# A prompt delta rule's triangular inverse: 32-blocks joined by 32x32 products in two column groups, and the last join sent to both column halves

## The chip, the cores and the metric

The kernel runs on one core of a Trainium2 chip. A core has TensorE (matrix products, results into PSUM), VectorE, ScalarE, GpSimd, and SyncE, which mostly issues DMAs. The metric is the time of one execution on the device in microseconds; the number compared is the median over runs. A profiled execution is one more run, recorded by the hardware profiler, and its own time differs a little from that of the timed runs.

## The reference

One decoder layer for a prompt of 1024 tokens and for 8 samples of 4 tokens: a combined projection, a stick-breaking attention (8 heads of 64) beside a gated delta rule (4 heads of 128), a merge, and a channel mixer. What matters here is the delta rule of the prompt. The reference works it out in chunks:

```python
def step(s, inp):
    qc, kc, vc, gc, bc = inp
    cg = jnp.cumsum(gc, axis=-1)
    decay = jnp.exp(jnp.where(incl, cg[..., :, None] - cg[..., None, :], -jnp.inf))
    m = jnp.where(strict, bc[..., :, None] * jnp.einsum('bhik,bhjk->bhij', kc, kc) * decay, 0.0)
    rhs = jnp.concatenate([vc * bc[..., None], kc * (bc * jnp.exp(cg))[..., None]], axis=-1)
    sol = lax.linalg.triangular_solve(eye + m, rhs, left_side=True, lower=True, unit_diagonal=True)
    u, w = sol[..., :d_v], sol[..., d_v:]
    v_new = u - jnp.einsum('bhck,bhkv->bhcv', w, s)
    ...
```

The solve with I + m, m strictly lower triangular, is the part that the change touches. All inputs and outputs are float32.

## The kernel before, in words

The prompt's 1024 tokens are 8 chunks of 128, and the kernel inverts I + M for a whole chunk of 128 at once, so that the solve becomes products. For each of the four heads (gdn_head, h from 0 to 3):

- Projections (proj, with its helper dense at lines 137 to 139) make k, q, v and the gate z of the head. Their matmuls are named pd_uk, pd_uq, pd_uv, pd_z.
- M for the 8 chunks stands in one tile (E1 in the code, E in the profile), 128 partitions by 8 x 128.
- The four diagonal 32x32 blocks of every chunk are inverted on VectorE by substitution (lines 471 and 473), in a layout that takes two trips through DRAM (tiles ms and tv). The result, block diagonal, comes back in t32 (t in the profile), and U is its transpose by blocks (line 491).
- The join from 32 to 64 is two steps. Step one (line 500) multiplies U's odd blocks by M under a mask (ml, line 495), full 128x128 products with 64 columns streamed, one per chunk; ScalarE copies the result out (xf, line 501). Step two (line 504) multiplies by t32 in the same form; VectorE subtracts the result from U (line 505), and a transpose and a copy (lines 507 and 508) bring the new block into t32.
- The join from 64 to 128 is steps three and four (lines 511 and 517): products of 64x64, all written to PSUM partitions 0 to 63, with ScalarE's copy x2 between (line 514) and VectorE's copy into U after (line 519).
- With U done, the chain over the 8 chunks follows (lines 526 to 555), the norm, the transposes t_o, the gating zl, and a store.

In the profile the four steps' PSUM tiles are all called l, and a float32 product appears as two MATMUL records.

The order of the instructions is not the order of the code. A planner at build time simulates the program with its own costs and fixes each engine's order; each engine then runs its queue in that order and waits by semaphores. So the matmuls of the next head's projections, and of the attention's (pd_aq, pd_ak, pd_av with their transposes t_nk, t_nv), stand between the steps of the joins on TensorE. PSUM is eight banks, two per pool: the joins take theirs from the pool psg, the projections from psd and psf. On VectorE, ql is the difference that empties a bank of the query projection; qe (cgb in the profile, line 488) is q times an exponential, whose tile is loaded by DMA after the tile's earlier contents, zl of the head before, were stored.

Of the kernel before, what the change touches and what calls it, by code (L numbers as in the profile page):

```python
# [8 lines left out]
F32 = mybir.dt.float32  # L9
# [4 lines left out]
ALU = mybir.AluOpType  # L14
# [4 lines left out]
P = 128  # L19
# [19 lines left out]
def hybrid_step(ctx, tc, x_prompt, x_sample, cache_k, cache_v, page_table, state_conv, state_ssm,  # L39
# [211 lines left out]
    lmask = gk.tile([P, P], F32, name="lmask")  # L251
    V.memset(lmask, 0.0)
    V.memset(lmask[32:64, 0:32], 1.0)
    V.memset(lmask[96:128, 64:96], 1.0)
# [125 lines left out]
    def c8(ap):  # L380
        return ap.rearrange("p (c f) -> p c f", f=P)

    def odd(ap):
        return ap.rearrange("p (a b f) -> p a b f", b=2, f=32)[:, :, 1, :]

    def gdn_head(h):
# [107 lines left out]
        ml = gk.tile([P, NC, P], F32, tag="ms", name=f"ml{h}")  # L494
        V.tensor_tensor(ml, c8(M), lmask.unsqueeze(1).to_broadcast([P, NC, P]), op=ALU.mult)
        xf = gk.tile([P, NP], F32, tag="tv", name=f"xf{h}")
        G.memset(xf, 0.0)
        p1 = gtile(f"l1{h}")
        for c, sl in enumerate(cs_):
            PE.matmul(p1[:, 64 * c:64 * c + 64], lhsT=ml[:, c, :], rhs=odd(U[:, sl]), start=True, stop=True)  # L500
        S_.activation(odd(xf), p1.rearrange("p (a f) -> p a f", f=32), AF.Copy)
        p2 = gtile(f"l2{h}")
        for c, sl in enumerate(cs_):
            PE.matmul(p2[:, 64 * c:64 * c + 64], lhsT=t32[:, sl], rhs=odd(xf[:, sl]), start=True, stop=True)
        V.tensor_tensor(odd(U), odd(U), p2.rearrange("p (a f) -> p a f", f=32), op=ALU.subtract)
# [3 lines left out]
        p3 = gtile(f"l3{h}")  # L509
        for c in range(NC):  # L510
            PE.matmul(p3[0:64, 64 * c:64 * c + 64], lhsT=M[64:128, c * P:c * P + 64], rhs=c8(U)[64:128, c, 64:128],
                      start=True, stop=True)
        x2 = gk.tile([64, 512], F32, tag="x2", name=f"x2{h}")
        S_.activation(x2, p3[0:64, :], AF.Copy)
        p4 = gtile(f"l4{h}")
        for c in range(NC):
            PE.matmul(p4[0:64, 64 * c:64 * c + 64], lhsT=c8(t32)[0:64, c, 0:64], rhs=x2[:, 64 * c:64 * c + 64],
                      start=True, stop=True)
        V.tensor_scalar(c8(U)[0:64, :, 64:128], p4[0:64, :].rearrange("p (a f) -> p a f", f=64), -1.0, None, op0=ALU.mult)
# [1143 lines left out]
```

## Time and profile before

| | |
|---|---|
| median of 3 runs | 1745.63 us (1745.23 to 1746.56) |
| profiled execution | 1754.63 us, span of its instructions 1752.9 us |
| TensorE busy | 1704.8 us, 97% of the span, 13902 records |
| VectorE, ScalarE, GpSimd busy | 1148.9, 783.2, 206.6 us |
| mean granted TensorE clock | 0.992 |

A busy TensorE in this table is a sum over records whose spans overlap, so it tells that the engine had work, not how fast it worked. PE is TensorE's matmul row, PEld its weight loads, DVE is VectorE, ACT ScalarE, POOL GpSimd. The names behind an instruction are its output and inputs; 64*64 is rows by columns of the weights.

### The profile page before, as it was taken

How to read it: one execution, taken by the hardware profiler on the slowest of the kernel's cores; microseconds unless marked ns; L12 is line 12 of the kernel's file. 1: busy time of each engine (PE TensorE's matmuls, PEld its weight loads, DVE VectorE, ACT ScalarE, POOL GpSimd, SP SyncE). 2: the span in 40 equal slices, each digit the busy share in tenths (PEclk: the TensorE clock that was granted, in tenths of full speed). 3: DMA queues.
4: the chain of work that ended last, by engine and by line, in shares of the span. 5: the costliest groups of instructions: out<-in, count | busy, mean ns of one | idle time of the engine just before them, and what ended most of it. 6: DMA issues, size and time to landing. Idle time of an engine off the chain costs nothing.

```text
span 1752.9 us, 34523 instructions
## 1 busy us (share of the span) xinstructions
PE 1704.8 (97%) x13902; PEld 1645.2 (94%) x13902; DVE 1148.9 (66%) x2299; ACT 783.2 (45%) x1554; POOL 206.6 (12%) x247
## 2 busy tenths in 40 slices
PE   7999999999998999999999999999999999999998
PEld 6999999999998787887989999999999999999998
DVE  6665677868224416658857487887777678788843
ACT  5553435343323225555433355554544564444353
POOL 1110111110004125335310000000000000000000
PEclk9999999999998999999999999999999999999999
DMA  5142232234337457758223644554443666532321
GB/s 177 37 127 67 67 117 79 81 96 144 118 97 230 138 161 210 188 145 248 67 86 117 194 126 146 164 150 148 146 150 133 212 215 220 170 123 90 128 83 66
DMA packets 234219, 239.22 MB, mean 136 GB/s; under 512 B 22882, under 2 KB 192195, under 8 KB 234060
## 3 DMA queue, kind: packets, MB, share of 16 engines
q1 hardware_dynamic: 229110, 226.27, 42.4%
q0 software_dynamic: 3200, 10.52, 1.9%
q8 instruction: 109, 1.79, 0.4%
q10 hardware_dynamic: 1750, 0.23, 0.1%
q14 instruction: 50, 0.41, 0.1%
HBM read 163.21 MB, written 73.77 MB: 135 GB/s over the span
## 4 chain that ended last, share of the span: by engine, by line
PE 74%; issue 8%; DMA 6%; DVE 6%; POOL 3%; ACT 1%; SPq 1%; POOLq 0%; DVEq 0%; ACTq 0%
PE pu L139 6%; PE pu L137 6%; PE pu L138 6%; PE pw L139 4%; PE pw L138 4%; PE pw L137 4%; PE pd_g L137 2%; POOL am L938 2%; PE pd_g L139 2%; PE pd_g L138 2%; POOL s L935 1%; PE px L138 1%; PE px L137 1%; PE px L139 1%; PE pv L137 1%
## 5 line engine op out<-in xcount | busy, mean ns | idle before, releaser
L139 PE MATMUL pu<-Xh,ul 128*128 128x264 f32 x812 | 230.1, 284 | 0.0
L137 PE MATMUL pu<-Xh,uh 128*128 128x264 f32 x812 | 229.8, 283 | 0.1
L138 PE MATMUL pu<-Xl,uh 128*128 128x264 f32 x812 | 229.7, 283 | 0.0
L137 PE MATMUL pw<-hc,w 128*128 128x264 f32 x728 | 205.4, 285 | 2.4 <-ACT w L1475 2.4
L138 PE MATMUL pw<-hc,w 128*128 128x264 f32 x728 | 205.7, 286 | 0.0
L139 PE MATMUL pw<-hc,w 128*128 128x264 f32 x728 | 200.9, 285 | 1.0 <-DVE w L1476 1.0
L137 PEld LDWEIGHTS pu<-Xh,uh 128*128 128x128 f32 x812 | 153.1, 189 | 0.3 <-ACT uh L1226 0.3
L137 PE MATMUL pd_g<-xh,wh_g 128*128 128x256 f32 (+1 forms) x512 | 150.9, 295 | 1.8 <-ACT gt L1037 1.6
L138 PEld LDWEIGHTS pu<-Xl,uh 128*128 128x128 f32 x812 | 152.7, 188 | 0.0
L139 PEld LDWEIGHTS pu<-Xh,ul 128*128 128x128 f32 x812 | 152.0, 188 | 0.0
L139 PE MATMUL pd_g<-xh,wl_g 128*128 128x256 f32 (+1 forms) x512 | 149.2, 291 | 0.1
L138 PE MATMUL pd_g<-xl,wh_g 128*128 128x256 f32 (+1 forms) x512 | 148.6, 290 | 0.0
L137 PEld LDWEIGHTS pw<-hc,w 128*128 128x128 f32 x728 | 137.9, 190 | 2.6 <-ACT w L1475 2.6
L138 PEld LDWEIGHTS pw<-hc,w 128*128 128x128 f32 x728 | 137.2, 189 | 0.0
L139 PEld LDWEIGHTS pw<-hc,w 128*128 128x128 f32 x728 | 134.4, 188 | 1.4 <-DVE w L1476 1.4
L942 DVE TENSOR_TENSOR_SCAN pr<-am 128x127 f32<-128x127 f32 (+7 forms) x64 | 88.1, 1378 | 54.8 <-POOL am L938 54.8
L137 PEld LDWEIGHTS pd_g<-xh,wh_g 128*128 128x128 f32 x512 | 97.8, 191 | 7.0 <-ACT gt L1037 3.0
L139 PEld LDWEIGHTS pd_g<-xh,wl_g 128*128 128x128 f32 x512 | 97.6, 191 | 2.0 <-issue 1.9
L138 PEld LDWEIGHTS pd_g<-xl,wh_g 128*128 128x128 f32 x512 | 97.6, 191 | 0.6 <-issue 0.4
L1475 ACT ACTIVATE w<-a 128x512 fp32r<-128x512 f32 x78 | 43.5, 620 | 84.5 <-PE pw L139 74.4
L139 PE MATMUL px<-mh,wl_wo 128*128 128x264 f32 x256 | 72.2, 285 | 0.9 <-DVE wl_wo L1227 0.8
L138 PE MATMUL px<-ml,wh_wo 128*128 128x264 f32 x256 | 72.6, 285 | 0.0
(584 smaller groups left out, 5126.2 us busy)
## 6 DMA issues: line engine op xcount, KB each, us to landing
hc_d<-t SPq DMA_DIRECT2D x26, 924.0 KB
hc<-hc_d SPq DMA_DIRECT2D x87, 264.0 KB
a<-in_w_down_dram SPq DMA_DIRECT2D x48, 256.0 KB
ws_g<-in_w_in_dram SPq DMA_DIRECT2D x16, 512.0 KB
ws_wo<-in_w_o_dram SPq DMA_DIRECT2D x32, 256.0 KB
ua<-in_w_up_dram SPq DMA_DIRECT2D x16, 512.0 KB
ub<-in_w_up_dram SPq DMA_DIRECT2D x16, 512.0 KB
gA_d<-gt SPq DMA_DIRECT2D x8, 528.0 KB
```

The source lines that it names most:

```text
L137: PE.matmul(pt[:, :n], lhsT=wh[k], rhs=xh[k], start=(k == 0), stop=False)
L138: PE.matmul(pt[:, :n], lhsT=wh[k], rhs=xl[k], start=False, stop=False)
L139: PE.matmul(pt[:, :n], lhsT=wl[k], rhs=xh[k], start=False, stop=(k == nk - 1))
L935: G.affine_select(s[:, qsl], s[:, qsl], pattern=[[-1, P]], compare_op=ALU.is_gt, fill=0.0, base=0, channel_multiplier=1)
L938: G.tensor_scalar(am[:, :n], s[:, :n], -1.0, 1.0, op0=ALU.mult, op1=ALU.add)
L942: V.tensor_tensor_scan(pr[:, n - 1:0:-1], am_r, am_r, 1.0, op0=ALU.mult, op1=ALU.bypass)
L1475: S_.activation(tl[:, 0], src, AF.Copy)
```

## The change

Steps one and two become products of 32x32: per chunk two of them, one for each half of 64, with weights in row groups 1 and 3 (step one) or 0 and 2 (step two), written to PSUM partitions 0 to 31 and 64 to 95, which are column groups 0 and 2. The mask and the masked copy of M go, and so does the memset of xf. The copies between the steps become two of 32 partitions each. Steps three and four keep their 64x64 products but write even chunks to PSUM partitions 0 to 63 and odd chunks to 64 to 127; their copies become two as well.

```diff
-        ml = gk.tile([P, NC, P], F32, tag="ms", name=f"ml{h}")
-        V.tensor_tensor(ml, c8(M), lmask.unsqueeze(1).to_broadcast([P, NC, P]), op=ALU.mult)
-        xf = gk.tile([P, NP], F32, tag="tv", name=f"xf{h}")
-        G.memset(xf, 0.0)
-        p1 = gtile(f"l1{h}")
-        for c, sl in enumerate(cs_):
-            PE.matmul(p1[:, 64 * c:64 * c + 64], lhsT=ml[:, c, :], rhs=odd(U[:, sl]), start=True, stop=True)
-        S_.activation(odd(xf), p1.rearrange("p (a f) -> p a f", f=32), AF.Copy)
-        p2 = gtile(f"l2{h}")
-        for c, sl in enumerate(cs_):
-            PE.matmul(p2[:, 64 * c:64 * c + 64], lhsT=t32[:, sl], rhs=odd(xf[:, sl]), start=True, stop=True)
-        V.tensor_tensor(odd(U), odd(U), p2.rearrange("p (a f) -> p a f", f=32), op=ALU.subtract)
+        xf = gk.tile([P, NC, 32], F32, tag="tv", name=f"xf{h}")
+        p1, p2 = gtile(f"l1{h}").rearrange("p (c f) -> p c f", f=64), gtile(f"l2{h}").rearrange("p (c f) -> p c f", f=64)
+        halves = [(slice(64 * a, 64 * a + 32), slice(64 * a + 32, 64 * a + 64)) for a in range(2)]
+        for c in range(NC):
+            for ra, rb in halves:
+                PE.matmul(p1[ra, c, 0:32], lhsT=c8(M)[rb, c, ra], rhs=c8(U)[rb, c, rb], start=True, stop=True)
+        for ra, rb in halves:
+            S_.activation(xf[ra], p1[ra, :, 0:32], AF.Copy)
+        for c in range(NC):
+            for ra, rb in halves:
+                PE.matmul(p2[ra, c, 0:32], lhsT=c8(t32)[ra, c, ra], rhs=xf[ra, c, :], start=True, stop=True)
+        for ra, rb in halves:
+            V.tensor_scalar(c8(U)[ra, :, rb], p2[ra, :, 0:32], -1.0, None, op0=ALU.mult)
...
+        def at(pt, c):
+            return pt[64 * (c % 2):64 * (c % 2) + 64, 64 * (c // 2):64 * (c // 2) + 64]
+
+        def both(pt, r):
+            return pt[64 * r:64 * r + 64, 0:256].rearrange("p (c f) -> p c f", f=64)
+
+        def every(ap, r):
+            return ap.rearrange("p (c r) f -> p r c f", r=2)[:, r]
...
-            PE.matmul(p3[0:64, 64 * c:64 * c + 64], lhsT=M[64:128, c * P:c * P + 64], rhs=c8(U)[64:128, c, 64:128],
-                      start=True, stop=True)
-        x2 = gk.tile([64, 512], F32, tag="x2", name=f"x2{h}")
-        S_.activation(x2, p3[0:64, :], AF.Copy)
...
+            PE.matmul(at(p3, c), lhsT=M[64:128, c * P:c * P + 64], rhs=c8(U)[64:128, c, 64:128], start=True, stop=True)
+        for r in range(2):
+            S_.activation(every(x2, r), both(p3, r), AF.Copy)
         for c in range(NC):
-            PE.matmul(p4[0:64, 64 * c:64 * c + 64], lhsT=c8(t32)[0:64, c, 0:64], rhs=x2[:, 64 * c:64 * c + 64],
-                      start=True, stop=True)
-        V.tensor_scalar(c8(U)[0:64, :, 64:128], p4[0:64, :].rearrange("p (a f) -> p a f", f=64), -1.0, None, op0=ALU.mult)
+            PE.matmul(at(p4, c), lhsT=c8(t32)[0:64, c, 0:64], rhs=x2[:, c, :], start=True, stop=True)
+        for r in range(2):
+            V.tensor_scalar(every(c8(U)[0:64, :, 64:128], r), both(p4, r), -1.0, None, op0=ALU.mult)
```

Since the planner orders the engines, the change also moves work that it doesn't name. On TensorE, in the projection of the next head's k, step two of head 0 stood like this before (l is its PSUM tile, xf and t its inputs):

```order
L138 MATMUL pd_uk_2_2465<-xl_170,wh_uk_2409 128x256
L139 MATMUL pd_uk_2_2465<-xh_169,wl_uk_2410 128x256
L504 MATMUL l_1242<-xf_1230,t_1202 128x64 x8
L137 MATMUL pd_uk_2_2465<-xh_169,wh_uk_2409 128x256
L138 MATMUL pd_uk_2_2465<-xl_170,wh_uk_2409 128x256
```

and stands like this now, where line 498 is step two:

```order
L139 MATMUL pd_uk_2_2495<-xh_169,wl_uk_2440 128x256
L137 MATMUL pd_uk_2_2495<-xh_169,wh_uk_2439 128x256
L498 MATMUL l_1226<-xf_1224,t_1198 32x32
L138 MATMUL pd_uk_2_2495<-xl_170,wh_uk_2439 128x256
L498 MATMUL l_1226<-xf_1224,t_1198 32x32 x15
L139 MATMUL pd_uk_2_2495<-xh_169,wl_uk_2440 128x256
```

The block of 8 has become one product, a dense matmul, and 15 products. Step two of head 3 and step four of heads 1, 2 and 3 (line 522) are parted in the same way, with 1 to 18 dense matmuls between the first product and the others.

On TensorE around step one of head 2, before (t_o are the transposes of the head before, t_nv those of the attention's v, pd_aq the attention's query projection):

```order
L111 MATMUL t_o_1_2389<-ident,nw_2164 128x128 x2
L111 MATMUL t_nv_0_5381<-ident,vf_5268 128x128 x4
L500 MATMUL l_3106<-U_3099,ml_3102 128x64 x8
L111 MATMUL t_nv_1_5386<-ident,vf_5268 128x128 x4
L137 MATMUL pd_aq_0_5403<-xh_173,wh_aq_5399 128x256
```

and now, with step one at line 493:

```order
L139 MATMUL pd_av_3_5417<-xh_167,wl_av_5336 128x288
L111 MATMUL t_nv_0_5445<-ident,vf_5332 128x128 x4
L493 MATMUL l_3133<-U_3129,E_2943 32x32 x16
L111 MATMUL t_nv_1_5450<-ident,vf_5332 128x128 x4
L498 MATMUL l_3134<-xf_3132,t_3106 32x32 x16
L137 MATMUL pd_aq_0_5467<-xh_173,wh_aq_5463 128x256
```

Step two, which stood 22 dense matmuls behind those transposes, now follows them at once, and 19 dense matmuls of the projection pd_av have come between the transposes t_o and step one. From there to the first matmul of pd_aq's third chunk there were 48 dense matmuls before and are 67 now, and the first product of step four stands among them.

## Rows read from the trace of the kernel before

**Rows 1.** The table of busy times by stretch, for 40 to 530 us; the columns are the stretch, its length, busy us and count of PE, PEld, DVE, ACT and POOL, the granted TensorE clock as a share, the DMA share and GB/s.

```profile
40.00:530.00 490.00, 482.34 (x4021) 476.93 (x4020) 301.65 (x736) 193.53 (x435) 55.28 (x52) 1.00 0.31 93
```

**Rows 2.** What TensorE waited for from 60 to 530 us: us in total, times, longest.

```profile
PE pd_aq L137 <- DVE ql L794: 2.4, 1, 2.4
PE pd_uv L137 <- ACT upv L346: 1.1, 1, 1.1
PE t_nk L111 <- ACT ntk L804: 1.1, 2, 0.9
PE s L544 <- DVE y L540: 1.1, 1, 1.1
PE l L500 <- DVE U L491: 0.9, 1, 0.9
PE pd_av L137 <- DVE ksT L798: 0.6, 1, 0.6
PE wt L527 <- DVE kb L526: 0.2, 1, 0.2
```

**Rows 3.** The instructions that write or read U: steps one and three, with duration in ns (least, median, most), first and last start, and form.

```profile
L500 PE MATMUL l<-U,ml x64: 220/275/294, 163.8 to 445.3; 128*128 128x64 f32 x64
...
L511 PE MATMUL l<-U,E x64: 218/218/267, 173.7 to 454.6; 64*64 64x64 f32 x64
```

**Rows 4.** TensorE in order of time around step one of head 0: start, us to the end of the last, instruction, count.

```profile
163.72 0.28 PE L138 MATMUL pd_uk<-xl,wh_uk 128*128 128x256 f32 x1
163.84 1.90 PE L500 MATMUL l<-U,ml 128*128 128x64 f32 x16
...
165.75 0.28 PE L137 MATMUL pd_uk<-xh,wh_uk 128*128 128x256 f32 x1
165.86 0.28 PE L138 MATMUL pd_uk<-xl,wh_uk 128*128 128x256 f32 x1
```

**Rows 5.** The same around step three of head 0.

```profile
173.34 0.30 PE L137 MATMUL pd_uk<-xh,wh_uk 128*128 128x288 f32 x1
173.48 0.29 PE L138 MATMUL pd_uk<-xl,wh_uk 128*128 128x288 f32 x1
173.71 1.14 PE L511 MATMUL l<-U,E 64*64 64x64 f32 x16
...
175.01 0.30 PE L137 MATMUL pd_uk<-xh,wh_uk 128*128 128x288 f32 x1
```

**Rows 6.** The same view, cut to stretches inside steps one and three of head 0, so that only whole records at the running pace are in a row.

```profile
163.90 1.61 PE L500 MATMUL l<-U,ml 128*128 128x64 f32 x13
...
173.87 0.86 PE L511 MATMUL l<-U,E 64*64 64x64 f32 x12
```

**Rows 7.** Products on parts of the array elsewhere in the kernel. First the views by tile, with durations in ns (least, median, most): the decode's dks on four column groups, dav with 32x32 weights on four, dst with 32 rows on four row groups. Then rows in order of time, cut to the first few records of a block: dks, its weight loads, dav, dst, and the attention's po, which alternates between two column halves.

```profile
L723 PEld LDWEIGHTS dks<-sst,kz x128: 106/110/155, 555.4 to 575.5; 128*32 128x32 f32 x128
L723 PE MATMUL dks<-sst,kz x128: 269/273/421, 555.4 to 575.6; 128*32 128x128 f32 x128
...
L893 PE MATMUL dav<-vs_nat,dwn x16: 587/600/612, 620.4 to 639.2; 32*32 32x512 f32 x16
...
L766 PE MATMUL dst<-vexp,dkp x16: 587/640/692, 591.6 to 607.1; 32*128 32x512 f32 x16
...
572.13 0.32 PE L723 MATMUL dks<-sst,kz 128*32 128x128 f32 x4
...
572.13 0.13 PEld L723 LDWEIGHTS dks<-sst,kz 128*32 128x32 f32 x4 [0.17 <-issue]
...
620.38 0.63 PE L893 MATMUL dav<-vs_nat,dwn 32*32 32x512 f32 x4
...
591.63 0.70 PE L766 MATMUL dst<-vexp,dkp 32*128 32x512 f32 x2
...
694.71 1.53 PE L980 MATMUL po<-wt,vn 128*64 128x128 f32 x24
...
694.71 0.14 PEld L980 LDWEIGHTS po<-wt,vn 128*64 128x64 f32 x2 [0.17 <-issue]
```

**Rows 8.** Copies out of PSUM: the present ones of step one (ScalarE) and step two (VectorE) by tile, and copies of 256 elements a partition by line (busy us, mean ns).

```profile
L501 ACT ACTIVATE xf<-l x4: 579/598/600, 165.8 to 448.0; 128x512 f32<-128x512 f32 x4
...
L505 DVE TENSOR_TENSOR U<-U,l x4: 680/689/690, 170.6 to 450.7; 128x512 f32<-128x512 f32 x4
...
L346 ACT ACTIVATE upv<-pd_uv 128x256 f32<-128x256 f32 x12 | 4.3, 380 | 11.1 <-PE pd_uv L139 11.1
...
L794 DVE TENSOR_TENSOR ql<-pd_aq,qh 128x256 f32<-128x256 f32 x15 | 6.2, 413 | 3.9 <-ACT qh L792 3.7
```

**Rows 9.** The wait beside head 2: the last transposes t_o on TensorE, the DMA that loads cgb (from the chain of work), TensorE when it resumes, and the granted clock from 364 to 368 us.

```profile
351.43 0.38 PE L111 MATMUL t_o<-ident,nw 128*128 128x128 f32 x2
...
355.42 5.50 DMA cgb<-cg_d
...
365.44 0.58 PE L137 MATMUL pd_aq<-xh,wh_aq 128*128 128x256 f32 x1 [2.41 <-DVE ql L794]
365.82 0.41 PE L138 MATMUL pd_aq<-xl,wh_aq 128*128 128x256 f32 x1
...
368.17 0.37 PE L137 MATMUL pd_aq<-xh,wh_aq 128*128 128x256 f32 x1
...
364.00:368.00 4.00, 2.56 (x12) 2.56 (x13) 3.90 (x7) 1.32 (x4) 0.00 (x0) 0.62 0.02 4
```

More of the change, by code (lines that the diff above doesn't have):

```diff
@@ L249, in hybrid_step @@
     gk = pool("gk", stack=gctx, side="right")
[L251 to L254, printed above, removed]
     sel4 = gk.tile([P, P], F32, name="sel4")
@@ L381, in c8 @@
         return ap.rearrange("p (c f) -> p c f", f=P)
-    def odd(ap):
-        return ap.rearrange("p (a b f) -> p a b f", b=2, f=32)[:, :, 1, :]
     def gdn_head(h):
@@ L508, in gdn_head @@
         V.tensor_copy(c8(t32)[32:64, :, 0:32], tz)
-        p3 = gtile(f"l3{h}")
-        for c in range(NC):
-            PE.matmul(p3[0:64, 64 * c:64 * c + 64], lhsT=M[64:128, c * P:c * P + 64], rhs=c8(U)[64:128, c, 64:128],
-                      start=True, stop=True)
-        x2 = gk.tile([64, 512], F32, tag="x2", name=f"x2{h}")
-        S_.activation(x2, p3[0:64, :], AF.Copy)
-        p4 = gtile(f"l4{h}")
+        p3, p4 = gtile(f"l3{h}"), gtile(f"l4{h}")
+        x2 = gk.tile([64, NC, 64], F32, tag="x2", name=f"x2{h}")
+        def at(pt, c):
[4 more added lines that the diff above has]
+            return ap.rearrange("p (c r) f -> p r c f", r=2)[:, r]
+        for c in range(NC):
+            PE.matmul(at(p3, c), lhsT=M[64:128, c * P:c * P + 64], rhs=c8(U)[64:128, c, 64:128], start=True, stop=True)
+        for r in range(2):
+            S_.activation(every(x2, r), both(p3, r), AF.Copy)
         for c in range(NC):
-            PE.matmul(p4[0:64, 64 * c:64 * c + 64], lhsT=c8(t32)[0:64, c, 0:64], rhs=x2[:, 64 * c:64 * c + 64],
-                      start=True, stop=True)
-        V.tensor_scalar(c8(U)[0:64, :, 64:128], p4[0:64, :].rearrange("p (a f) -> p a f", f=64), -1.0, None, op0=ALU.mult)
+            PE.matmul(at(p4, c), lhsT=c8(t32)[0:64, c, 0:64], rhs=x2[:, c, :], start=True, stop=True)
+        for r in range(2):
+            V.tensor_scalar(every(c8(U)[0:64, :, 64:128], r), both(p4, r), -1.0, None, op0=ALU.mult)
         for hf in range(2):
```

## The prediction

> **What bounds the kernel now.** I read first the table of stages. From 40 to 530 us, where the four prompt heads run, TensorE is busy 482.3 of 490 us while VectorE has 301.7 and ScalarE 193.5 [rows 1]. Next the waits of TensorE alone from 60 to 530 us: seven kinds, 7.4 us in all, the longest 2.4 us [rows 2]. So TensorE's own work sets the time of this stage. The projections of the next head and of the attention fill it while a join waits for a copy. What a join costs TensorE is therefore paid almost in full, and its latency on the other engines is hidden as long as enough projection matmuls are planned behind it.
>
> Then the joins themselves. Each f32 product leaves two records, so a step of 8 products shows 16; 64 records over four heads for each of the four steps [rows 3]. Durations overlap, so I price a block of 16 by where its neighbours start. The first step of head 0 stands between a dense matmul at 163.72 and one at 165.75, which is 2.03 us for the block and two dense matmuls of 0.12 us: the block costs 1.79 us [rows 4]. The third step (64x64) stands between 173.48 and 175.01, 1.53 us with two dense matmuls of 0.133: 1.26 us [rows 5]. Inside a block the starts are regular: (1.61 - 0.275)/12 = 111.3 ns for 128 weight columns, (0.86 - 0.218)/11 = 58.4 ns for 64 [rows 6, 3]. 16 x 58.4 ns is 0.93 us, so 0.33 us of the third step is the price of entering and leaving a smaller tile: the first start comes 0.23 us after its predecessor instead of 0.133, and the next dense pair is as late again [rows 5].
>
> **The change, part by part.**
>
> *Steps one and two, from 128x128 to pairs of 32x32.* Before: 8 blocks x 1.79 = 14.3 us. After, a block has 16 products, 32 records, two column groups in turn. Do two groups run side by side? Four products on four groups start so close that all four together last 0.32 us where one lasts 0.27, and their weight loads together 0.13 where one lasts 0.11 [rows 7]; four of 32x32 take 0.63 us together against about 0.59 for one [rows 7]. They do, so a block is 16 paired steps. No row shows a step of 32 columns that is bound by 32. From 111.3 to 58.4 ns, 64 columns fewer save 52.9 ns; 32 fewer save 26.5: an estimate of 31.9 ns a step. Bounds: no gain over the 64-wide step and no overlap, 117 ns; below, starts a few ns apart, 14 ns. I take 31.9, since the row nearest in shape (32x32) shows full overlap. Block: 0.33 + 16 x 0.0319 = 0.84 us. Saved: 8 x (1.79 - 0.84) = 7.6 us (bounds -3.3 and +9.9).
>
> The rows show neighbouring groups start within (0.32 - 0.27)/3, under 20 ns [rows 7]. The Trainium skill has a rule against that: the page "TensorE: Matmul & The Clock Gate", section "Wait — 56ns, not 53.3ns?", says start to start never falls below about 25 ns. By it a step of two would be 50 ns, the saving would be 5.3 us and the time 1738.0. The trace disagrees with the rule for different column groups.
>
> The sum stays with 31.9 ns; a step twice as wide is a rival below.
>
> *Steps three and four, both column halves in turn.* The 16 records become 8 paired steps. The attention's products on two 64-column halves show it: 24 records in 1.53 us, (1.53 - 0.273)/23 = 55 ns apiece although each streams 128 columns, and two weight loads in 0.14 us [rows 7]. With 64 columns streamed the step stays at 58.4 ns for two. Saved: 8 blocks x 8 x 58.4 ns = 3.7 us; bounds 0 (halves in series) and 3.7.
>
> *Order.* The planner now splits five of sixteen blocks into one product, some dense matmuls, and the rest: step two in heads 0 and 3, step four in heads 1, 2 and 3. Each split enters and leaves the small tile once more, 0.33 us, and two products lose their partner: two steps more, 0.06 us at 32 wide and 0.12 us at 64 wide. Cost: 5 x 0.33 + 2 x 0.06 + 3 x 0.12 = 2.1 us (bounds 0.5, if a lone product hardly drains, and 3).
>
> *Copies and cover.* The copies out of PSUM become two each: ScalarE 0.59 us to about 2 x 0.38, VectorE 0.69 to at most 2 x 0.42 [rows 8]; the masked M on VectorE and a memset on GpSimd go. None of this is on TensorE. Its cover is the dense matmuls between two steps, some 23 x 0.12 = 2.8 us in head 0, against a latency of about 1.0 us (0.28 us to drain, two copies of 0.38). With head 2 the cover between steps one and two shrinks to four transposes (4 x 0.11 us, [rows 9]), with head 3 the first product of step two has no more: I put a wait of 0.5 us and 0.3 us there. Were the cover gone everywhere, four heads would pay 0.5 us each.
>
> *The one large wait.* Beside head 2 TensorE stands 2.41 us before the third chunk of a query projection: its PSUM bank is freed by ql, which stands on VectorE behind the product with cgb, which waits for its exponential, for a DMA of 5.50 us, and for the store of zl [rows 9]. From the last t_o transpose (351.43) to the resumption (365.44) this is 14.0 us that the change doesn't shorten. Between the two TensorE had 14.0 - 2.4 = 11.6 us of work. It has now 19 dense matmuls more (2.5 us) and one product of step four (0.4), the 0.5 us wait, and 2.4 us less in joins: about 12.6 us, so the wait falls from 2.4 to about 1.4, a gain of 1.0 us. After it the granted clock was 1.2 GHz for a while: mean 0.62 from 364 to 368 us, 11 dense starts in 2.35 us instead of 1.3 [rows 9], some 1.1 us. I leave that in both and keep it for the range.
>
> *Other lines.* The three removed memsets and the mask's first part lie at the start beside other VectorE work: nothing. Behind the heads the order of TensorE's rows is the same but for a few rows in the channel mixer, so the later stages only begin earlier.
>
> *Sum.* -7.6 - 3.7 + 2.1 - 1.0 + 0.3 = -9.9 us, against the profiled execution of 1754.63 us: 1744.7. The timed runs have a median of 1745.63, 9.0 us below the profiled one; the saving is work and not share, so I take it off unchanged: **1735.7 us**.
>
> **Rivals.**
>
> *A paired step costs about 60 ns, not 32.* Either the two halves run in series (here they use different row groups too and write the same PSUM bank), or a step keeps the 58.4 ns of the 64-wide tile. For: no row before has two row groups writing one bank; the decode's rows with two row groups that start together (two in 0.70 us, one lasts about 0.64) write different banks [rows 7]. Against: those rows, and the four 32x32 products side by side. Price: in series 8 x 16 x 31.9 ns = 4.1 us, 1739.8; at 58.4 ns 8 x 16 x 26.5 ns = 3.4 us, 1739.1. I take 1739.8. The Trainium skill, "TensorEngine Tiling (Array Packing)", section "Gotcha 1: PSUM Pressure", says that different row tiles cannot use one bank at the same time; no run here shows it yet.
>
> *The saved work comes back as waits.* In heads 1 to 3 a chain such as that of cgb is as long as before; if TensorE reaches its foot with no filler left, it gives back what it saved in that head's first three steps, 2 x 0.95 + 0.47 = 2.4 us each, 7.2 us: 1742.9. For: the wait of 2.41 us. Against: the rest of the waits is 5 us in 470, and the planner added filler just there.
>
> *Slower: tile switching and small steps win.* If nothing overlaps and every record keeps the 64-wide 58.4 ns, steps one and two cost 0.33 + 32 x 0.0584 = 2.20 us, 0.41 more than before, 3.3 us in all; steps three and four give nothing; the splits cost 1.7 and waits give back 0.7: +4.3, 1749.9. The point that decides: with the other terms as forecast, a paired step of 109 ns or more in steps one and two. For: a block of 16 at 64x64 lasts 0.05 us longer than its cadence gives, 1.14 - 0.218 against 15 x 0.0584 [rows 5], so a step that doesn't follow another like it is dear. Against: every row of a running cadence.
>
> *The new order makes a new stall* of the kind in head 2, 2.4 us and 1.1 us of low clock, in each of three heads, against the gain: +0.6, 1746.2. The traces show one such stall in four heads.
>
> **How the numbers follow.** Forecast 0.56, steps of 60 ns 0.19, waits 0.13, slower by small steps 0.05, new stalls 0.07. What a measurement of this kernel tells from no change is about 0.2%, 3.5 us. Faster (below 1742.1): the forecast, the steps of 60 ns, and a third of the waits, 0.79; within: most of the waits, half of the new stalls, 0.13; slower: 0.08. The forecast's own range is 1732 to 1739 (splits, the low clock, the step's width). The range to give: 1731.5, steps at the lower bound and the low clock gone, to 1743.5, which takes in both first rivals.
>
> **What would show it.** Steps one and two as blocks of 32 records in about 0.8 us, starts in pairs some 32 ns apart; 64 ns would mean series. Steps three and four in about 0.8 us, half a microsecond less than now. TensorE's first dense matmul behind each block 0.1 us late, at splits twice. The wait before the third chunk of the query projection beside head 2 under 2 us. Stages from 530 us on of the same length as before. Wrong would be: joins cheaper as priced, and yet the stage to 530 us as long, with longer waits in the table of waits.

## The result, and the profile after

The changed kernel took 1736.3 us against 1745.43 us for the kernel before, ratio 0.9943, interval 0.9929 to 0.9957. Two later comparisons of the same two kernels gave 0.9944 [0.9929, 0.996] (1736.91 against 1747.26) and 0.9921 [0.9895, 0.9946] (1742.4 against 1755.7). The forecast was 1735.7 us, 9.9 us less; by the medians, 9.1, 10.4 and 13.3 us less were measured. The kernel before ran at 1745 to 1747 us in some sets of runs and at 1754 to 1756 in others, so only times of one set are compared below. The later sets ran on three different chips, one set on each: 1753.66 us on the first, 1747.26 on the second, 1755.7 on the third. Whether it is the chip that sets the level, these runs can't tell. The first profile of the kernel before (1754.63 us) is like the slower sets; the step between the first two profiled spans, 1752.9 to 1735.2, is therefore larger than what the medians show.

First the line of busy times of the page, whole program, of the changed kernel, and its stretch from 40 to 530 us (columns as in [rows 1]):

```profile
PE 1689.5 (97%) x14030; PEld 1631.0 (94%) x14030; DVE 1143.6 (66%) x2300; ACT 781.7 (45%) x1560; POOL 198.2 (11%) x243
...
40.00:530.00 490.00, 484.18 (x4254) 476.24 (x4253) 308.71 (x780) 199.50 (x452) 57.95 (x55) 1.00 0.35 104
```

The stage is as full as before, and more of the program's work fits into it. TensorE still bounds it. What it waited for from 60 to 530 us, the answer to [rows 2]:

```profile
PE t_nk L111 <- ACT ntk L809: 1.7, 2, 1.0
PE pd_uv L137 <- ACT upv L342: 1.1, 1, 1.1
PE t_nv L111 <- ACT ntv L809: 0.7, 1, 0.7
PE pd_uk L137 <- ACT upk L342: 0.7, 1, 0.7
PE pd_uk L139 <- DVE wl_uk L128: 0.7, 1, 0.7
```

The wait for ql, 2.4 us and the longest before, is gone. The waits for ntk and ntv have grown. All waits of TensorE in this stretch together are 5.8 us, for 7.4 before. The blocks themselves, the answer to [rows 4] and [rows 5]: TensorE in order of time around step one (L493) and step three (L518) of head 0.

```profile
164.76 0.28 PE L138 MATMUL pd_uk<-xl,wh_uk 128*128 128x256 f32 x1
164.97 0.69 PE L493 MATMUL l<-U,E 32*32 32x32 f32 x32
165.60 0.39 PE L139 MATMUL pd_uk<-xh,wl_uk 128*128 128x256 f32 x1
165.82 0.28 PE L137 MATMUL pd_uk<-xh,wh_uk 128*128 128x256 f32 x1
...
172.95 0.29 PE L138 MATMUL pd_uk<-xl,wh_uk 128*128 128x288 f32 x1
173.17 0.68 PE L518 MATMUL l<-U,E 64*64 64x64 f32 x16
173.78 0.40 PE L139 MATMUL pd_uk<-xh,wl_uk 128*128 128x288 f32 x1
174.02 0.30 PE L137 MATMUL pd_uk<-xh,wh_uk 128*128 128x288 f32 x1
```

From the dense matmul ahead to the second one behind it is 1.06 us at step one, less two usual distances of 0.12: 0.82 us for the block (0.84 forecast, 1.79 before). At step three it is 1.07 less 0.27: 0.80 us (1.26 before). The pace inside comes from the same view cut at two places in each block:

```profile
164.97 0.28 PE L493 MATMUL l<-U,E 32*32 32x32 f32 x6
164.97 0.63 PE L493 MATMUL l<-U,E 32*32 32x32 f32 x28
...
173.17 0.33 PE L518 MATMUL l<-U,E 64*64 64x64 f32 x4
173.17 0.62 PE L518 MATMUL l<-U,E 64*64 64x64 f32 x14
```

22 records more take 0.35 us, 15.9 ns each and 32 ns a pair of records, one of each column group; 10 records more of 64x64 take 0.29 us, 58 ns a pair. Forecast were 31.9 and 58.4.

### The profile page after: what moved, and what is told of

It reads as the page before. It is cut to its first block, busy times and chain, and to the rows that moved or that the text cites. A ratio compares the mean times of both kernels' runs of the same rounds, so it can differ in the third digit from the quotient of the medians.

```text
span 1735.2 us, 34777 instructions
## 1 busy us (share of the span) xinstructions
PE 1689.5 (97%) x14030; PEld 1631.0 (94%) x14030; DVE 1143.6 (66%) x2300; ACT 781.7 (45%) x1560; POOL 198.2 (11%) x243
## 4 chain that ended last, share of the span: by engine, by line
PE 77%; DVE 6%; issue 6%; DMA 6%; POOL 3%; ACT 2%; SPq 0%; POOLq 0%; DVEq 0%; ACTq 0%
PE pu L139 6%; PE pu L137 6%; PE pu L138 6%; PE pw L139 4%; PE pw L138 4%; PE pw L137 4%; PE pd_g L137 2%; PE pd_g L139 2%; PE pd_g L138 2%; POOL am L943 2%; PE px L138 1%; PE px L137 1%; PE px L139 1%; PE pv L139 1%; PE pv L137 1%
```

## The experiments

One column of the table needs a word. "Joins" is the sum over the 16 blocks of the distance from the dense start ahead to the second start behind, less the usual distances, so waits that stand right at a block are in it. Idle is the span less TensorE's busy time; a moment in which several records overlap counts once as busy.

| kernel | median, us | before in that set | ratio | span | PE busy | idle | joins |
|---|---|---|---|---|---|---|---|
| before, first profile | 1745.43 | | | 1752.9 | 1704.8 | 48.1 | 28.2 |
| before, second profile | 1753.55 | 1753.66 | 0.9997 | 1755.1 | 1704.6 | 50.5 | 29.9 |
| changed, first profile | 1736.3 | 1745.43 | 0.9943 | 1735.2 | 1689.5 | 45.7 | 17.4 |
| changed, second | 1736.91 | 1747.26 | 0.9944 | 1735.8 | 1690.0 | 45.8 | 17.4 |
| changed, third | 1742.4 | 1755.7 | 0.9921 | 1739.5 | 1693.2 | 46.3 | 17.4 |
| first join only | 1748.49 | 1753.66 | 0.9963 | 1750.9 | 1702.0 | 48.9 | 20.9 |
| second join only | 1749.1 | 1753.66 | 0.9967 | 1747.9 | 1700.2 | 47.7 | 23.1 |
| one to two in series | 1748.1 | 1747.26 | 1.0008 | 1746.5 | 1698.6 | 47.9 | 22.3 |
| one and three in series | 1745.42 | 1755.7 | 0.9934 | 1744.6 | 1697.3 | 47.3 | 18.9 |
| late half first, two and four | 1751.26 | 1753.66 | 0.9986 | 1747.3 | 1695.3 | 52.0 | 16.0 |
| late half first, two | 1744.26 | 1755.7 | 0.9927 | 1743.2 | 1694.8 | 48.4 | 16.5 |
| changed, zl in U's buffer | 1745.11 | 1747.26 | 0.9987 | 1743.6 | 1692.5 | 51.1 | 16.7 |
| late half first, zl in U's buffer | 1749.37 | 1747.26 | 1.0013 | 1744.8 | 1688.0 | 56.8 | 13.9 |
| before, zl in U's buffer | 1770.08 | 1755.7 | 1.0075 | 1766.4 | 1703.1 | 63.3 | 24.3 |

**The kernel before, profiled again.** No edit.

> The kernel before, unchanged, for a second profile of it. The theory that the change is worth what its blocks cost on TensorE (about 10 us) says that this execution's span lies near 1743 us, 9 to 10 us under the first profile's 1752.9, so that the step from the first profile to the changed one (17.7 us) is half the change and half the luck of one execution; the extra 9 us should then lie in stretches that the change doesn't touch (stalls after head 3, 540 to 660 us). The rival, that the change is worth 17 us in every execution and the median times hide it, says a span near 1752 again. Ratio 1.000 within 0.0015 by both.

Its median was 1753.55 us, ratio 0.9997 [0.9982, 1.0012], and its span 1755.1. The expectation of a span near 1743 fell. The rival's span of about 1752 came out within 3 us, but not for its reason, since the medians never showed 17 us: it is the sets of runs, not single executions, that are 8 us apart. The stalls of the decode stage were there again (dks 3.8 us, 4.2 in the first profile), so they belong to this order of instructions.

**The two halves of the change, each alone.** The first has steps one and two of the changed kernel and steps three and four of before:

```diff
-        for c, sl in enumerate(cs_):
-            PE.matmul(p1[:, 64 * c:64 * c + 64], lhsT=ml[:, c, :], rhs=odd(U[:, sl]), start=True, stop=True)
+        for c in range(NC):
+            for ra, rb in halves:
+                PE.matmul(p1[ra, c, 0:32], lhsT=c8(M)[rb, c, ra], rhs=c8(U)[rb, c, rb], start=True, stop=True)
```

> Only steps one and two (32 to 64) as in the changed kernel, steps three and four as before. If what counts is the time of the blocks on TensorE: eight blocks of 32x32 at 0.81 us for 1.77 us, less 0.4 us for the one block that the program's order splits: 7.3 us less than before, ratio 0.9958. If the saved time comes back as waits for ScalarE's copies: under 3 us less, ratio over 0.998. If the changed kernel's gain comes mostly from other places that moved along (the wait beside head 2): this edit alone gives any ratio, and the wait for ql beside head 2, 2.41 us before, tells: gone if this edit moves head 2 early enough.

The ratio was 0.9963 [0.9949, 0.9976], 6.5 us by the ratio and 5.2 by the medians; the 7.3 expected lie within the interval. The blocks of steps one and two took 0.82 us where no wait or cut stood beside them. A new wait came beside head 3, 2.4 us for zl. The wait for ql is down to 0.7 us, though the edit touches nothing in the chain that leads to it: another order did that.

The second has steps three and four of the changed kernel and steps one and two of before:

```diff
-            PE.matmul(p3[0:64, 64 * c:64 * c + 64], lhsT=M[64:128, c * P:c * P + 64], rhs=c8(U)[64:128, c, 64:128],
-                      start=True, stop=True)
+            PE.matmul(at(p3, c), lhsT=M[64:128, c * P:c * P + 64], rhs=c8(U)[64:128, c, 64:128], start=True, stop=True)
```

> Only steps three and four (64 to 128) as in the changed kernel, steps one and two as before. If what counts is the time of the blocks: eight blocks at 0.80 us for 1.26 us, less 0.4 us for the one block that is split: 3.3 us less than before, ratio 0.9981, blocks of 0.8 us with pairs starting 58 to 59 ns apart. If waits take it back: ratio 0.9995 to 1.001. By the first theory the gains of this run and of the run of the first join add up to the changed kernel's, after its four more splits (1.6 us) are taken off.

The ratio was 0.9967 [0.9955, 0.9979], 5.8 us by the ratio (3.7 to 7.9) and 4.6 by the medians, where 3.3 were expected. Six of the uncut blocks took 0.80 to 0.81 us as expected, one 0.87. The rest fits the wait for ql, which isn't in the list of waits of this kernel (2.4 and 2.6 us in the two profiles of before). Together the halves are worth 12.3 us by their ratios and 9.7 by their medians, about the changed kernel's 9 to 13. The changed kernel itself wasn't timed in this set. The blocks alone give the first half about its size and the second too little: a wait that goes or comes beside a block is as large as that gap.

**Is it the overlap?** First both of steps one and two in series:

```diff
-        for c in range(NC):
-            for ra, rb in halves:
+        for ra, rb in halves:
+            for c in range(NC):
                 PE.matmul(p1[ra, c, 0:32], lhsT=c8(M)[rb, c, ra], rhs=c8(U)[rb, c, rb], start=True, stop=True)
```

and the same for p2.

> The changed kernel, but steps one and two issue the eight products of one half and then the eight of the other, so that neighbours stand in the same row group and column group. If two products in different groups run beside each other and that is what pays: starts 32 ns apart without the 6 to 7 ns partner, 32 records of a block for 1.02 us in place of 0.51, blocks of 1.3 us in place of 0.8, eight times 0.5: 4.1 us more than the changed kernel (ratio to before 0.997). If the small products alone pay (fewer rows and columns, no overlap needed): blocks of 0.8 us still and the changed kernel's time.

The ratio was 1.0008 [0.9996, 1.002], 11.2 us more than the changed kernel in the same set, where 4.1 were expected. Blocks took 1.22 us, so eight of them explain 3.2 us. But reversing the loops also changed when step two's first product is ready, and with it the order of the whole program: beside the blocks there were new waits of 2.1 us (qsT) and 2.0 us (U). This run mixes two causes, so a cleaner one followed: steps one and three alone in series, where every engine's instructions stand in the same order as in the changed kernel, but for two neighbours on VectorE that changed places.

```diff
-        for c in range(NC):
-            for ra, rb in halves:
+        for ra, rb in halves:
+            for c in range(NC):
                 PE.matmul(p1[ra, c, 0:32], lhsT=c8(M)[rb, c, ra], rhs=c8(U)[rb, c, rb], start=True, stop=True)
...
-        for c in range(NC):
+        for c in (0, 2, 4, 6, 1, 3, 5, 7):
             PE.matmul(at(p3, c), lhsT=M[64:128, c * P:c * P + 64], rhs=c8(U)[64:128, c, 64:128], start=True, stop=True)
```

> The changed kernel with steps one and three alone in series: the eight products of one half, then those of the other, so that the partner in the other column group is 8 (4) products away. Steps two and four as they are, and the order in which every engine's instructions stand is the same as in the changed kernel. If the overlap of the two column groups is what pays, and time on TensorE in these blocks is paid in full when the order is kept: step one's blocks 1.3 us for 0.80 and step three's 1.25 for 0.80, 4 x 0.50 + 4 x 0.45 = 3.8 us more than the changed kernel, with the same waits. If the surrounding waits absorb it: 0 to 1.5 us more, the waits for ntk and ntv behind step one shorter by as much.

It took 1745.42 us beside 1742.4 for the changed kernel in this set: 3.0 us more. The ratios, 0.9934 [0.9909, 0.9958] and 0.9921 [0.9895, 0.9946], overlap, but they carry the scatter of the kernel before. Beside each other the two separate: the six runs of this kernel took 1744.83 to 1746.71 us, five of the six of the changed kernel 1741.21 to 1742.64 and one 1745.9. The trace shows where. Step one of head 0, the same cut inside the block, step three of head 0, and step one of heads 2 and 3 with what follows it:

```profile
164.17 1.09 PE L493 MATMUL l<-U,E 32*32 32x32 f32 x32
...
164.17 0.53 PE L493 MATMUL l<-U,E 32*32 32x32 f32 x11
...
172.77 0.96 PE L518 MATMUL l<-U,E 64*64 64x64 f32 x16
...
347.64 1.09 PE L493 MATMUL l<-U,E 32*32 32x32 f32 x32
349.05 0.33 PE L111 MATMUL t_nv<-ident,vf 128*128 128x128 f32 x1 [0.31 <-ACT ntv L809]
...
432.64 1.09 PE L493 MATMUL l<-U,E 32*32 32x32 f32 x32
434.31 0.66 PE L111 MATMUL t_nk<-ident,kf 128*128 128x128 f32 x4 [0.58 <-ACT ntk L809]
```

Against the same places of the changed kernel in heads 2 and 3 (for head 0 see the section on the result):

```profile
347.55 0.69 PE L493 MATMUL l<-U,E 32*32 32x32 f32 x32
348.95 0.66 PE L111 MATMUL t_nv<-ident,vf 128*128 128x128 f32 x4 [0.71 <-ACT ntv L809]
...
432.58 0.69 PE L493 MATMUL l<-U,E 32*32 32x32 f32 x32
434.25 0.66 PE L111 MATMUL t_nk<-ident,kf 128*128 128x128 f32 x4 [0.98 <-ACT ntk L809]
```

Three things are to be seen. In series the first 11 records take 0.53 us; less the 0.19 that one record lasts, that is 34 ns a start, the longer first step included, where two shared 32 ns: the overlap of the two halves is real and worth half of the running time. The block grew from 0.69 to 1.09 us, 0.40 us more, not the 0.50 expected: 32 records at 32 ns would take 31 x 0.032 + 0.19 = 1.18 us, so at the joint the second half's first records run beside the first half's last ones. Step three's block grew by 0.28 us (0.96 for 0.68) for the 0.45 expected, for the same reason. And the 0.40 us is paid in heads 0 and 1 only. In head 2 the wait for ntv behind the block shrinks from 0.71 to 0.31 us, exactly as much as the block grew. Head 3 does the same, its wait for ntk goes from 0.98 to 0.58. So both theories hold, each at its place: 2 x 0.40 + 4 x 0.28 = 1.9 us paid, 0.8 us absorbed; the other 1.1 us of the 3.0 are not accounted for. The series block also parts the gain of steps one and two: priced like the others it costs 1.22 us, so of the 0.97 us from 1.79 to 0.82 the smaller products alone give 0.57 and the overlap 0.40.

**The cuts.** Five of the changed kernel's blocks have their first product planned ahead of the others, with dense matmuls between. Step two of head 0, in order of time:

```profile
168.33 0.28 PE L137 MATMUL pd_uk<-xh,wh_uk 128*128 128x256 f32 x1
168.54 0.24 PE L498 MATMUL l<-xf,t 32*32 32x32 f32 x2
168.71 0.39 PE L138 MATMUL pd_uk<-xl,wh_uk 128*128 128x256 f32 x1
169.03 0.69 PE L498 MATMUL l<-xf,t 32*32 32x32 f32 x30
169.65 0.39 PE L139 MATMUL pd_uk<-xh,wl_uk 128*128 128x256 f32 x1
```

The first product needs the first copy only, its partner the second. If the one that needs the second copy is issued first, all are ready together:

```diff
-            for ra, rb in halves:
+            for ra, rb in halves[::-1]:
                 PE.matmul(p2[ra, c, 0:32], lhsT=c8(t32)[ra, c, ra], rhs=xf[ra, c, :], start=True, stop=True)
...
-        for c in range(NC):
+        for c in (1, 0, 3, 2, 5, 4, 7, 6):
             PE.matmul(at(p4, c), lhsT=c8(t32)[0:64, c, 0:64], rhs=x2[:, c, :], start=True, stop=True)
```

> The changed kernel with the products of steps two and four in another order: in each pair the one that needs the second copy goes first, so that no block is cut in two in the program's order. If each cut costs two more changes of shape on TensorE and a lost partner (blocks of 0.45+0.89, 0.36+0.80, 0.82+0.78, 0.44+0.79 and 0.53+0.88 us in the changed kernel): all eight blocks of steps two and four take 0.8 us, the five cuts' 2.5 us go, 1733.8 us, ratio to before 0.993. If the cut only filled time in which TensorE would have waited for the second copy: blocks of 0.8 us, but as much more wait ahead of them, and the time stays at 1736.3, ratio 0.9947.

The cuts went, seven of the eight blocks took 0.80 to 0.82 us, the joins fell to 16.0 us, and the gain went too: ratio 0.9986 [0.9967, 1.0004]. Neither theory had that. The two largest waits of TensorE from 60 to 530 us, 5.5 us that the changed kernel hasn't, and ScalarE and VectorE beside head 2 show where most of it went:

```profile
PE pd_ak L137 <- DVE ql L799: 3.4, 1, 3.4
PE l L493 <- DVE zl L575: 2.1, 1, 2.1
...
362.88 1.28 ACT L480 ACT_TABLE_LOAD   x1 [5.13 <-DMA cgb<-cg_d]
...
365.26 1.22 DVE L481 TENSOR_TENSOR cgb<-cvq,cgb 128x1024 f32<-128x1024 f32 x1 [8.53 <-ACT cgb L480]
```

This is the chain of [rows 9] again, and longer: ScalarE stands 5.1 us for the load of the row into cgb, VectorE 8.5 us for ScalarE, and ql behind it 3.4 us late for TensorE. In this order VectorE takes the products with zl behind the transpose of U; in the changed kernel they stand ahead of it. The buffer's store and the next load start that much later.

So step two alone was reversed, which leaves zl ahead of U's transpose:

```diff
-            for ra, rb in halves:
+            for ra, rb in halves[::-1]:
                 PE.matmul(p2[ra, c, 0:32], lhsT=c8(t32)[ra, c, ra], rhs=xf[ra, c, :], start=True, stop=True)
```

> The changed kernel with the late half first in step two alone: the two cuts of step two (heads 0 and 3) go, and the order in which VectorE takes zl and the transpose of U beside head 2 stays as in the changed kernel, which the version with both steps reversed had turned round. If a cut costs what its block shows (0.45+0.89 and 0.36+0.80 for 0.80 each) and that version lost by the turned order: 0.5 to 1.0 us less than the changed kernel and no wait for ql beside head 2. If taking the cuts away loses by itself: 5 us or more slower than the changed kernel again.

No wait for ql, as expected; the joins fell by 0.9 us to 16.5, as expected; the time did not: 1744.26 us beside 1742.4, intervals that overlap. The cuts' price inside the blocks is shown. That removing them makes the kernel faster is not.

**Is that load the cause?** The row for qe and zl share a buffer. With zl in the buffer of U, whose contents are used up by then, the load needn't wait for the store of zl. But the edit does a second thing, which neither expectation has: U of the next head is now written into the buffer that zl leaves, and has to wait for that store.

```diff
-        zl = gk.tile([P, NP], F32, tag="cgb", name=f"zl{h}")
+        zl = gk.tile([P, NP], F32, tag="U", name=f"zl{h}")
```

In the changed kernel:

> The changed kernel with zl in U's buffer, so that the row that qe is made of (tile cgb) is loaded without waiting until zl has been stored. The changed kernel has no wait for ql beside head 2, only DVE's waits for ScalarE's exp of that row (10.1 us in four). If only waits of TensorE count: within 1.5 us of the changed kernel, better or worse by the order alone. If DVE's and ScalarE's blocked queues cost TensorE time in general: 2 to 4 us less than the changed kernel.

and in the one with the late half first:

> The kernel with the late half first (no block cut in two), which had 3.4 us of wait for ql and 2.1 us for zl beside heads 2 and 3 and was 2.4 us under before only, with zl in U's buffer as well. If the load of qe's row behind the store of zl is what held ScalarE (5.1 us), VectorE (8.5 us) and through ql TensorE (3.4 us): that wait goes, the blocks stay at 0.8 us, and the ratio to before is 0.992 (12 to 14 us less). If the loss of that kernel has another cause: ratio 0.997 to 0.999 again.

Both expectations failed. The first was 8.2 us slower than the changed kernel in its set (0.9987 [0.9972, 1.0003] to before). The second had the cheapest joins of all, 13.9 us, and was not faster than before: 1.0013 [1.0001, 1.0025]. In it the wait for ql beside head 2 is gone, which fits the load as its cause, though the order around it changed as well. But another wait for ql, 2.1 us, stood beside head 1 in both kernels. In the second, VectorE stood 8.6 us before the transpose that writes U, for the store of zl (the first line, from the view of that transpose), and these waits and this stretch stood at the first scores:

```profile
  DMA o_d<-zl: 8.6, 2
...
PE sc L937 <- DMA kh<-kh_d: 12.0, 1, 12.0
...
640.00:650.00 10.00, 0.32 (x3) 0.11 (x1) 0.00 (x0) 0.38 (x1) 0.00 (x0) 0.71 1.06 254
```

TensorE is busy 0.32 us of these ten: the first scores wait 12 us for the load of kh, while the DMA engines are full (share 1.06). These loads are issued right behind the store of the decode's output, osT, at 639.3 us here, and the first scores come 13 us later. In the changed kernel the store is issued at 620.4 and the first scores come at 635.9, no sooner; but 121 products of the gate's projection fill those 15 us, as the view by tile between the two shows, first for the changed kernel:

```profile
L139 PE MATMUL pd_g<-xh,wl_g x41: 279/285/300, 620.8 to 635.7; 128*128 128x256 f32 x25, 128*128 128x288 f32 x16
L137 PE MATMUL pd_g<-xh,wh_g x40: 279/285/297, 620.9 to 635.5; 128*128 128x256 f32 x24, 128*128 128x288 f32 x16
L138 PE MATMUL pd_g<-xl,wh_g x40: 279/284/296, 621.1 to 635.6; 128*128 128x256 f32 x24, 128*128 128x288 f32 x16
```

and for this one:

```profile
L137 PE MATMUL pd_g<-xh,wh_g x3: 280/281/282, 639.1 to 639.8; 128*128 128x256 f32 x3
L138 PE MATMUL pd_g<-xl,wh_g x3: 279/282/285, 639.2 to 639.9; 128*128 128x256 f32 x3
L139 PE MATMUL pd_g<-xh,wl_g x3: 278/279/281, 639.3 to 640.0; 128*128 128x256 f32 x3
```

Nine. The filler had been placed earlier. An order that is cheaper in one stage can leave the next one without cover.

**The same edit of the buffer in the kernel before.** It changes no product and no copy:

> The kernel before with zl in U's buffer, an edit that changes no product and no copy, only when the row for qe can be loaded. If the order that the program takes after any edit is worth up to 10 us by itself: a time that differs from the kernel before by 3 to 10 us either way, with TensorE's time in the joins unchanged (22.6 us) and the difference in waits and in the filling of the stretch before the first scores. If order is worth little: within 1.5 us of before, and the wait for ql gone (2.4 us).

The ratio was 1.0075 [1.0049, 1.01], 14.4 us slower by the medians, with TensorE's busy time 1.5 us lower than in the second profile of before. No wait stood beside a block: the joins are 24.3 us, where 22.6 were expected.

The largest waits of this kernel:

```profile
PE sc L932 <- DMA kh<-kh_d: 11.4, 1, 11.4
...
PE t_nv L111 <- ACT ntv L804: 5.0, 3, 3.0
```

The same 11 us at the first scores, and 5 us at the transposes of nv; a wait of 1.6 us for ql stood beside head 1. The waits after the edit of one buffer are worth more than the whole change. What order alone is worth, the run doesn't show, because the edit also delays U: VectorE writes it at 261.4, 365.9 and 461.6 us in heads 1 to 3, for 246.8, 337.9 and 442.2 in the kernel before. The 11 us come long after that, at scores that read neither U nor zl, and fit a filler placed elsewhere; for the rest order and the new wait can't be told apart.

**The changed kernel, repeated.** In two of the sets:

> The changed kernel again, beside the runs of this call. If the gain is the blocks and the wait for ql that this program's order avoids: ratio to before 0.994 to 0.995 again, no wait for ql beside head 2, and a span about 10 us under the kernel before profiled twice (1752.9 and 1755.1), so near 1744. If the gain in the first profile (17.7 us of span) is real in every execution: ratio 0.990.

> The changed kernel once more, as the measure for the other runs of this call: ratio to before 0.9944 within 0.0015, span 1735 to 1737 us if this chip is like the others.

The first ratio held, 0.9944; its span, 1735.8, was not near 1744 but like the first profile's. The second ratio, 0.9921, and its span, 1739.5, both missed what was expected of them, though the interval takes in 0.9944. The joins are 17.4 us in all three profiles and idle is 45.7 to 46.3 us, so these two belong to the program. TensorE's busy time is not so fixed: 1689.5, 1690.0, 1693.2. Put beside the first profile instruction by instruction, the third falls 8.5 us behind between 524 and 542 us, gets 5.8 back in the 10 us after, and loses 4.1 from 596 to 606. Among its waits there is a line that the first hasn't:

```profile
PE pd_g L138 <- issue: 2.7, 4, 1.1
```

## Why the prediction was right

*What bounds the kernel.* Right: the joins cost TensorE 28.2 us before and 17.4 after, 10.8 less, and the medians moved by 9 to 13.

*Steps one and two, -7.6.* Blocks of 0.84 us were forecast; the uncut blocks without a wait took 0.81 to 0.82, so 8 x (1.78 - 0.82) = 7.7 us is the size. The estimate of 31.9 ns for a paired step came out at 32. No row had shown a step of that width, so that it met the number so closely is in part luck. Step one of heads 2 and 3 leads into waits for ntv and ntk, where part of the saving was returned; that is counted with the new waits below.

*Steps three and four, -3.7.* 8 x (1.26 - 0.80) = 3.7. Right.

*The rival of the paired step at 60 ns* is out. The half that rested on one PSUM bank is settled too: both halves of p1 lie in one bank, the row groups differ, and a pair of records takes 32 ns, while in the series run each record needs 32 ns. *The rival that small steps make it slower* asked for 109 ns a step and is out by the same rows. The Trainium skill, "TensorEngine Tiling (Array Packing)", section "Gotcha 1: PSUM Pressure", says that row tiles cannot share a bank at one time; where the column groups differ as well, the trace disagrees. The floor of about 25 ns between starts in the Trainium skill ("TensorE: Matmul & The Clock Gate", section "Wait — 56ns, not 53.3ns?") isn't kept either: 15.9 ns a record on average.

*The cuts, +2.1.* Measured from the blocks: 0.54 and 0.36 in step two (0.45 + 0.89 and 0.36 + 0.80, less 0.80 each), 0.81, 0.43 and 0.62 in step four, 2.8 us, with 0.3 us of wait for wl_uq in the 0.81. Mis-sized by 0.7.

*The wait beside head 2, -1.0.* The step that failed: "From the last t_o transpose (351.43) to the resumption (365.44) this is 14.0 us that the change doesn't shorten." TensorE's own work on that way was forecast well, 12.6 us; from the last start of t_o to the third chunk it is 12.8 now. The chain beside it did get shorter. From the last start of t_o to the end of ql it was 13.9 us before and is 12.2 now. In the changed kernel these are the transposes, the load of cgb in the chain of work, ql, the third chunk's first matmul, and the stretch where TensorE had run at 1.2 GHz, now at 2.4 (granted clock 1.00 for 0.62):

```profile
L111 PE MATMUL t_o<-ident,nw x8: 270/271/275, 342.8 to 344.4; 128*128 128x128 f32 x8
...
348.45 3.75 DMA cgb<-cg_d
...
356.12 0.43 DVE L799 TENSOR_TENSOR ql<-pd_aq,qh 128x256 f32<-128x256 f32 x1
...
357.18 0.39 PE L137 MATMUL pd_aq<-xh,wh_aq 128*128 128x256 f32 x1
...
364.00:368.00 4.00, 4.00 (x34) 3.79 (x32) 3.93 (x7) 1.93 (x3) 0.00 (x0) 1.00 0.31 125
```

The load took 3.75 us for the 5.50 of [rows 9], which is the whole difference. Before, a load of 512 KB into ws_av was issued 1.7 us ahead of it; in the new order that load is issued 1.3 us behind it. That this made it shorter fits, but wasn't tried by itself. So ql is done 0.6 us before TensorE comes to the third chunk. The whole 2.4 us went, and the 1.1 us of low clock with it: 3.5 us for 1.0.

*The new waits, +0.3.* They came behind step one of heads 2 and 3, where they were forecast, and larger: ntk 1.7 for 1.1 before, ntv 0.7 for none, +1.3 us. They are put down to ntv and ntk, which ScalarE takes ahead of xf, and not to xf itself.

These terms give -7.7 - 3.7 + 2.8 - 3.5 + 1.3 = -10.8. The forecast's -9.9 was met partly because the errors of the small terms cancel, which is luck. That the joins fell by 10.8 too is no proof of the sum: most of the 1.1 us of low clock lies outside them, and smaller waits came and went that the sum leaves out.

*The rival of the saved work coming back as waits*, 7.2 us in heads 1 to 3, didn't come true: the waits named above took back 1.3 us, and all of TensorE's waits from 60 to 530 us fell by 1.6.

*"Behind the heads ... the later stages only begin earlier."* This was the weak sentence. From 530 to 660 us the changed kernel waits for other things than the one before:

```profile
PE sc L937 <- ACT s L939: 6.8, 1, 6.8
PE dkt L111 <- DMA kg<-in_cache_k_dram,idx: 3.4, 1, 3.4
...
540.00:550.00 10.00, 6.63 (x76) 5.18 (x75) 1.64 (x3) 3.04 (x5) 4.90 (x4) 0.82 0.77 240
```

These 10.2 us are new; 4.2 us at dks, 2.3 at xrp and 1.6 at pd_g are gone. The stretches at 1.2 GHz only moved: the granted clock was 0.51 from 560 to 570 us before, and is 0.82 and 0.84 in the two stretches of 10 us from 540 us and 0.77 and 0.89 in the two from 640 us. Up to the first product of px, the output projection, both kernels have done the same work outside the joins. The changed one comes to it at 935.8 us and the one before at 952.2, 16.4 us earlier, of which the joins give 10.8; from there on both take the same time, 799 and 801 us. So in the two profiles the stages between the heads and px gained some 6 us that the medians of the first two comparisons don't show. That was not foreseen, and the spread between profiles of one program, above, is as large.

*The rival of new stalls* was priced at one stall like head 2's in each of three heads, 1746.2, with a chance of 0.07. It didn't come true in the heads of this kernel; behind them new stalls of 10 us came, and others went. The variants lost 7 to 14 us: with the late half first, with zl in U's buffer, in the series run, where 3.2 us of it are the blocks. Part of their stalls stood outside the heads, where the prediction hadn't looked. The price was too small; whether the chance was, one kernel doesn't tell.

What stays open: why the kernel before runs 8 us apart in different sets of runs, where chip and set can't be told apart, and why TensorE's busy time differs by 3.7 us between profiles of one program. What share the planned order has in the 9 to 13 us is open too; only the run with steps one and three in series kept it. The cost of the half clock in the decode stage wasn't tried by itself.

## What to carry to other kernels

Price a block of small matmuls by the starts of its dense neighbours and by the step inside it, never by its busy time; here that gave each uncut block to 0.04 us. On a planned order, the edit's own cost is only one of two terms: an edit of one buffer without any arithmetic moved this kernel by 14 us, through a new dependency and the order that was planned around it. So a kernel that is 10 us faster is a finding about its order too, and each variant of it has to be timed again. Before an edit is called neutral, ask what the buffer's next owner now waits for. To test one cost, find an edit that leaves every engine's order as it is, and look behind the block: a wait that shrinks by what the block grew tells that the saving there was never paid.

## What the runs showed of the hardware

Products in two column groups overlap fully although they write one PSUM bank: a pair of records starts every 32 ns at 32x32, where the row groups differ too, and every 58 ns at 64x64, where the rows are the same (a float32 product is two records). In series each record needs 32 or 58 ns by itself, except where one group's list ends and the other's begins; there they ran beside each other without being interleaved in the program, so a block in series took 1.09 us in place of the 1.18 that its pace gives. A lone product between dense matmuls is dear: one 32x32 product and its way in and out cost 0.36 to 0.45 us where the whole block of 16 costs 0.82.
